# Rounded tile sizes and a written start order in a two-layer trunk kernel

## The chip, the cores and the metric

The kernel runs on one core of one Trainium2 chip. The metric is the device time of one execution in microseconds (us), as the median of several runs.

## The reference

`x` is 512 tokens of 1024 channels in fp32. Two residual layers follow each other. The first mixes tokens by a gated short convolution beside forgetting attention, the second by a conformer convolution module; a SwiGLU block follows each. Every sub-layer is normed ahead and behind. What the change touches is the beginning of the first mixer, cut here to its lines:

```python
def rms_norm(x, g):
    y = xf * lax.rsqrt(jnp.mean(xf * xf, axis=-1, keepdims=True) + RMS_EPS)
    return y * g

u = rms_norm(h, norm_mix_pre[layer])
proj = u @ w_in                      # gate B | gate C | xa | q | k | v | forget
log_f = log_sigmoid(proj[..., OFF_F:] + b_f)
y = concat([gate_b * conv3(gate_c * xa), attention(q, k, v, log_f)]) @ w_out
h = h + rms_norm(y, norm_mix_post[layer])
h = h + rms_norm(swiglu_ffn(rms_norm(h, norm_ffn_pre[layer])), norm_ffn_post[layer])
```

## The kernel before

Channels lie on the 128 partitions, eight tiles `h0` to `h7` of 128 x 512; tokens lie along the tile. Each fp32 factor is kept as a pair, a rounded high part and what is left (`xh` and `xl`, `wh` and `wl`), and each product is three matmuls (`mm3`, L198 to L200). The norm's factor per token isn't applied to `x` ahead of the product: `xh`, `xl` hold x times the gain, and the results are scaled by the factor later (`R`, spread over all partitions, and `rcol`, a column per 128 tokens).

Weights stream through `ensure` (L157 to L183): SyncE issues the transfer of a 512 KB chunk into `wr` (two buffers), ScalarE copies it rounded to `wh` (L176), and VectorE, for some chunks GpSimd, subtracts it for `wl` (L178, L181). For the first chunks of the start (`w_xa`) this is done in two halves.

The start of the program, in TensorE's order: `first()` has 32 units (k outer, four column blocks m inner) of three matmuls with `w_xa`; `forget()` has eight units of two matmuls (L425, L426) with the forget weights `wf`; `values()` has 32 units of three (L468 to L470) with `w_v`. Into this order `weave` puts other steps after a given number of units: `stats0` after STAT0 = 5 units of `forget()`, the norm's spread after STAT1 = 15 and the gate columns after GATES = 45. `stats0` sums the squares' columns with matmuls against a tile of ones (L258) in two halves of 256 tokens, each a group of two columns in the same PSUM bank `o`, the tag of which has one buffer. VectorE reads the two columns (L292, L293) and takes the root's inverse in Newton steps (L278, L283, L285). The squares are taken 256 wide on ScalarE (L248) and added 256 wide on GpSimd (L241).

TensorE's order is written by hand for the whole program. The order of ScalarE, VectorE, GpSimd and SyncE at the start is a scheduler's. In the later stages the tiles named `z` are streamed by TensorE too: they hold, among others, the hidden tiles of the SwiGLU blocks (outputs of L879 and its like). In the conformer stage (from 700 us) shifted copies of tiles are made by way of DRAM (`ct`, `uf`), and VectorE adds up the taps (L1015, L1132).

Tiles stand one behind the other in SBUF in the size that they ask for. Added up in that order, `xh`, `xl`, `wh`, `wl`, `wr` and `h` begin 64 bytes past a multiple of 128, the tiles `z0` to `z22`, `t` and `m` 32 bytes past it but for one.

Of the kernel before, what the change touches and what calls it, by code (L numbers as in the profile page):

```python
# [7 lines left out]
F32 = mybir.dt.float32  # L8
FR = mybir.dt.float32r
I32 = mybir.dt.int32  # L10
AF = mybir.ActivationFunctionType
ALU = mybir.AluOpType
AX = mybir.AxisListType

P = 128
T = 512
D = 1024
NK = D // P
NF = 22
HALF = NF // 2  # L20
TB = T // P
HT = T // 2
NH = 8
HD = 64
TAPS = 31
STAT0 = 5
STAT1 = 15
GATES = 45
LAG = 3
# [39 lines left out]
RMS_EPS = 1e-6  # L69
# [5 lines left out]
V_MIX_PRE = 0  # L75
# [14 lines left out]
def trunk(tc, x, vec, bands, w_xa, w_in, w_v, w_f, w_out, w_fi, w_fo, w_p1, w_p2, out):  # L90
# [5 lines left out]
    nc = tc.nc  # L96
    act = nc.scalar.activation
    tt = nc.vector.tensor_tensor
    ts = nc.vector.tensor_scalar
    stt = nc.vector.scalar_tensor_tensor  # L100
    mm = nc.tensor.matmul

    with tc.tile_pool(name="sb", bufs=1) as sb, tc.tile_pool(
        name="ps", bufs=1, space=bass.MemoryType.PSUM
    ) as pp, tc.tile_pool(name="dr", bufs=1, space=bass.MemoryType.DRAM) as dr:
        uid = [0]

        def alloc(tag, shape=(P, T), dt=F32, bufs=1):
            uid[0] += 1
            return sb.tile(list(shape), dt, name=f"{tag}_{uid[0]}", tag=tag, bufs=bufs)  # L110

        def psum(tag="g", shape=(P, T)):
            uid[0] += 1
            return pp.tile(list(shape), F32, name=f"p{tag}_{uid[0]}", tag=f"p{tag}", bufs=BANKS[tag])
# [5 lines left out]
        chunks = []  # L120
# [25 lines left out]
        for m in range(NK):  # L146
# [3 lines left out]
        count = {}  # L150
        pool_split = {(n, i) for n, w in (("p1", SPLIT1), ("p2", SPLIT2), ("in", SPLIT3), ("out", SPLIT4),
                                              ("fi", SPLIT5)) for i, c in enumerate(w) if c == "P"}
        split = []
        cursor = [0]
        spares = [None]

        def ensure(n, pieces=1):  # L157

            while len(split) < min(n, len(chunks)):
                name, ap, spare = chunks[len(split)]  # L160
                count[name] = count.get(name, -1) + 1
                raw = alloc("wr", (P, D), F32, 2)
                if spare is None:
                    h = alloc("wh", (P, D), FR, 5)
                    l = alloc("wl", (P, D), FR, 5)
                else:
                    if spare == 0:
                        spares[0] = alloc("pth", (P, 2560), FR), alloc("ptl", (P, 2560), FR)
                    h, l = (t[:, spare * D : (spare + 1) * D] for t in spares[0])
                a = ap.shape[1]  # L170
                r3 = raw.rearrange("p (a b) -> p a b", a=a)
                for i in range(pieces):
                    cs = slice(i * D // pieces, (i + 1) * D // pieces)
                    ps = slice(i * a // pieces, (i + 1) * a // pieces)
                    nc.sync.dma_start(r3[:, ps], ap[:, ps])
                    act(h[:, cs], raw[:, cs], AF.Copy)  # L176
                    if (name, count[name]) not in pool_split:
                        tt(out=l[:, cs], in0=raw[:, cs], in1=h[:, cs], op=ALU.subtract)  # L178
                        continue
                    for c in range(i * D // pieces, (i + 1) * D // pieces, HT):  # L180
                        nc.gpsimd.tensor_tensor(out=l[:, c : c + HT], in0=raw[:, c : c + HT], in1=h[:, c : c + HT],  # L181
                                                op=ALU.subtract)
                split.append((name, h, l))  # L183

        def take(name, ahead=2):
            i = cursor[0]
# [21 lines left out]
        ones = alloc("ones", (P, P), F32)  # L208
        nc.vector.memset(ones, 1.0)
        vecs = alloc("vecs", (P, NV), F32)  # L210

        def col(i, n=1):
            return vecs[:, i : i + n]
# [74 lines left out]
        def rsqrt_cols(sums, n, scale, eps):  # L288

            a = alloc("st_a", (P, 4), F32, 3)[:, :n]  # L290
            b = alloc("st_b", (P, 4), F32, 3)[:, :n]
            ts(out=a, in0=sums, scalar1=scale, scalar2=eps, op0=ALU.mult, op1=ALU.add)  # L292
            ts(out=b, in0=sums, scalar1=-0.5 * scale, scalar2=-0.5 * eps, op0=ALU.mult, op1=ALU.add)  # L293
            return newton(a, b, n)
# [31 lines left out]

        h = [alloc(f"h{k}") for k in range(NK)]
        nc.scalar.dma_start(vecs[:, : V_MIX_PRE + NK], vec[:, : V_MIX_PRE + NK])
        for k in range(NK):
            nc.sync.dma_start(h[k], x[:, k])  # L330
            if k % 2 == 0:
                ensure(k // 2 + 1, 2)
        wf_raw = slot(24, (P, NK * NH), F32)
        nc.sync.dma_start(wf_raw, w_f)
        nc.sync.dma_start(vecs[:, V_MIX_PRE + NK :], vec[:, V_MIX_PRE + NK :])
        wf = slot(25, (P, NK, 5, NH))

        def x_tiles():
# [5 lines left out]
            mm(warm[:, :P], ones, ones, start=True, stop=True)  # L344

        xh, xl = x_tiles()
        sums = Sums()
        for k in range(NK):
            g = col(V_MIX_PRE + k)
            ts(out=xh[k], in0=h[k], scalar1=g, scalar2=None, op0=ALU.mult)  # L350
            stt(out=xl[k], in0=h[k], scalar=g, in1=xh[k], op0=ALU.mult, op1=ALU.subtract)  # L351
            for hf in range(2):
                sums.square(hf, h[k][:, hf * HT : (hf + 1) * HT], k == NK - 1)
        wf3 = wf_raw.rearrange("p (k c) -> p k c", k=NK)
        act(wf[:, :, :4], wf3.unsqueeze(2).to_broadcast([P, NK, 4, NH]), AF.Copy)
        tt(out=wf[:, :, 4], in0=wf3, in1=wf[:, :, 0], op=ALU.subtract)
        R, R2 = alloc("R"), slot(23, dt=F32)
        rcol = alloc("rcol", (P, 4), F32)

        def stats0():  # L360
            for hf in range(2):
                nc.vector.tensor_copy(rcol[:, 2 * hf : 2 * hf + 2], rsqrt_cols(sums.cols(hf, "o"), 2, 1.0 / D, RMS_EPS))

        def stats1():
            act(R, spread(*each(rcol, 4)), AF.Copy)
# [14 lines left out]
        def first():  # L380

            ps = [psum("g") for _ in range(4)]
            for k in range(NK):
                if k % 2 == 0:
                    w = take("xa")
                for m in range(4):
                    mm3(ps[m], blk(w, k % 2 * 4 + m), (xh[k], xl[k]), k == 0, k == NK - 1)
                    yield
            for m in range(4):
                xa[m] = slot(2 * m, dt=F32)  # L390
                act(xa[m], ps[m], AF.Copy)
# [22 lines left out]
        def chain(*gens):  # L414
            for g in gens:
                yield from g
# [42 lines left out]
        def values():  # L459
            pv = [psum("g") for _ in range(TB)]  # L460
            for c in range(4):
                w = take("v")
                for j in range(2):
                    k = 2 * c + j
                    wh, wl = w[0][:, j * T : (j + 1) * T], w[1][:, j * T : (j + 1) * T]
                    for b in range(TB):
                        bs = slice(b * P, (b + 1) * P)
                        mm(pv[b], xh[k][:, bs], wh, start=k == 0, stop=False)  # L468
                        mm(pv[b], xh[k][:, bs], wl, start=False, stop=False)
                        mm(pv[b], xl[k][:, bs], wh, start=False, stop=k == NK - 1)  # L470
                        yield
            for b in range(TB):
                v4 = []
                for j in range(2):
                    w = slot(8 + 2 * b + j)
                    w4 = w.rearrange("p (e s d) -> p e s d", e=4, s=2)
                    p4 = pv[b][:, j * HT : (j + 1) * HT].rearrange("p (e d) -> p e d", e=4)
                    act(w4[:, :, 0], p4, AF.Copy, scale=rcol[:, b : b + 1])
                    stt(out=w4[:, :, 1], in0=p4, scalar=rcol[:, b : b + 1], in1=w4[:, :, 0],
                        op0=ALU.mult, op1=ALU.subtract)  # L480
                    v4.append(w)
                v.append(v4)
# [109 lines left out]
            stats1()  # L592
            gate_rows()

        weave(first())
        weave(chain(forget(), values()), [(STAT0, stats0), (STAT1, norm_known), (GATES, gate_cols)])

        def gemm_qk(i, j):
            return gemm("in", lambda ps: ev_qk(i, j, ps))
# [321 lines left out]
        g = {}  # L921
# [365 lines left out]
```

## Time and profile before

| | before |
|---|---|
| median of 3 runs | 1227.32 us (1225.16 to 1228.58) |
| profiled execution, its own time | 1230.15 us |
| span of the profiled execution | 1228.4 us |
| TensorE (PE) busy | 1178.8 us, 96% |
| VectorE (DVE) busy | 669.9 us, 55% |
| ScalarE (ACT) busy | 516.4 us, 42% |
| GpSimd (POOL) busy | 289.6 us, 24% |

The span runs from the first to the last instruction of the execution that was profiled; its own time lies 1.75 us above it. Busy is the time in which an engine works on some instruction. Matmuls overlap, so the distance between the starts of two of them tells more than the time of one.

### The profile page before, as it was taken

The page shows a single profiled execution, that of the slowest core. Times are in us where ns is not written, and L with a number is a line of the kernel's source. Part 1 is how long each engine was busy: PE and PEld are TensorE (multiplying, and loading weights), DVE is VectorE, ACT ScalarE, POOL GpSimd, SP SyncE. Part 2 cuts the span into 40 slices and gives each one's busy share as a digit, 9 for nine tenths or more (in the row PEclk, how much of TensorE's full clock was granted, in tenths as well). Part 3 has the DMA queues.
Part 4 walks back from the last instruction along what each step waited for, and adds up shares of the span by engine and source line. Part 5 has one row for each costly group of instructions (what it writes and reads, how often), then busy time and mean ns, then how long its engine had stood idle before and what let it go on. Part 6 is the DMA issues. An engine that isn't in the chain of part 4 may idle for free.

```text
span 1228.4 us, 16273 instructions
## 1 busy us (share of the span) xinstructions
PE 1178.8 (96%) x6134; PEld 997.8 (81%) x6134; DVE 669.9 (55%) x1240; ACT 516.4 (42%) x958; POOL 289.6 (24%) x373
## 2 busy tenths in 40 slices
PE   8899999989999999999999989899999999999994
PEld 6677777988888888888988878798888888888884
DVE  7568884375442234443378989827544323444416
ACT  4356774664232223322365664556433222332320
POOL 4244442741000000001545588046300000000010
PEclk9999999999999999999999999899999999999997
DMA  5332223414333233332313543022333323333212
GB/s 179 105 120 86 75 81 103 121 35 138 92 97 102 87 100 89 103 103 86 90 51 109 156 148 93 1 74 66 103 113 94 102 86 103 88 101 103 86 35 69
DMA packets 43118, 115.88 MB, mean 94 GB/s; under 512 B 4696, under 2 KB 14040, under 8 KB 43040
## 3 DMA queue, kind: packets, MB, share of 16 engines
q1 hardware_dynamic: 39936, 109.30, 29.9%
q10 hardware_dynamic: 2384, 3.15, 0.8%
q0 software_dynamic: 720, 2.39, 0.6%
q8 instruction: 48, 0.79, 0.3%
q14 instruction: 30, 0.25, 0.1%
HBM read 109.05 MB, written 5.78 MB: 93 GB/s over the span
## 4 chain that ended last, share of the span: by engine, by line
PE 75%; DVE 11%; DMA 4%; ACT 4%; POOL 3%; issue 3%; SPq 0%; DVEq 0%; ACTq 0%; POOLq 0%
PE pg L198 22%; PE pg L199 22%; PE pg L200 22%; DVE ps L1015 2%; PE pg L796 1%; PE pg L797 1%; DVE wl L178 1%; PE pp L561 1%; ACT wh L176 1%; DMA wr<-w_p 1%; POOL wl L181 1%; DMA wr<-w_fi 1%; POOL acc L241 1%; PE ps L540 1%; PE po L580 1%
## 5 line engine op out<-in xcount | busy, mean ns | idle before, releaser
L198 PE MATMUL pg<-xh,wh 128*128 128x512 f32 (+1 forms) x960 | 371.3, 387 | 0.1
L199 PE MATMUL pg<-xl,wh 128*128 128x512 f32 (+1 forms) x960 | 367.1, 382 | 3.1 <-DVE xl L351 3.1
L200 PE MATMUL pg<-xh,wl 128*128 128x512 f32 (+1 forms) x960 | 367.8, 383 | 1.0 <-DVE wl L178 1.0
L176 ACT ACTIVATE wh<-wr 128x1024 fp32r<-128x1024 f32 (+1 forms) x186 | 193.0, 1041 | 416.1 <-PE pg L199 331.0
L178 DVE TENSOR_TENSOR wl<-wr,wh 128x1024 fp32r<-128x1024 f32 (+1 forms) x145 | 176.1, 1216 | 178.5 <-ACT wh L176 178.0
L241 POOL TENSOR_TENSOR acc<-acc,sq 128x256 f32<-128x256 f32 x106 | 85.1, 815 | 720.5 <-ACT sq L248 719.2
L199 PEld LDWEIGHTS pg<-xl,wh 128*128 128x128 f32 x960 | 180.8, 188 | 37.6 <-DVE xl L351 3.8
L200 PEld LDWEIGHTS pg<-xh,wl 128*128 128x128 f32 x960 | 180.4, 188 | 37.6 <-DVE wl L178 2.0
L198 PEld LDWEIGHTS pg<-xh,wh 128*128 128x128 f32 x960 | 181.0, 189 | 34.5 <-issue 0.7
L198 PE MATMUL pg<-z,wh 128*128 128x512 f32 (+1 forms) x514 | 182.1, 354 | 0.0
L199 PE MATMUL pg<-z,wh 128*128 128x512 f32 (+1 forms) x514 | 181.0, 352 | 0.8 <-DVE z L411 0.8
L200 PE MATMUL pg<-z,wl 128*128 128x512 f32 (+1 forms) x514 | 181.1, 352 | 0.0
L181 POOL TENSOR_TENSOR wl<-wr,wh 128x256 fp32r<-128x256 f32 x164 | 132.7, 839 | 130.8 <-ACT wh L176 130.4
L199 PEld LDWEIGHTS pg<-z,wh 128*128 128x128 f32 x514 | 96.6, 188 | 15.6 <-DVE z L411 1.2
L198 PEld LDWEIGHTS pg<-z,wh 128*128 128x128 f32 x514 | 96.7, 188 | 14.7 <-ACT m L680 0.3
L200 PEld LDWEIGHTS pg<-z,wl 128*128 128x128 f32 x514 | 96.7, 188 | 14.4
L877 DVE TENSOR_TENSOR t<-pg,R 128x512 f32<-128x512 f32 (+1 forms) x48 | 31.0, 645 | 120.3 <-PE pg L200 120.3
L875 DVE TENSOR_TENSOR t<-pg,R 128x512 f32<-128x512 f32 (+1 forms) x48 | 31.0, 646 | 81.9 <-PE pg L200 79.4
L1015 DVE SCALAR_TENSOR_TENSOR ps<-z,vecs,ps 128x512 f32<-128x512 f32 x69 | 49.1, 750 | 0.6 <-ACT ps L1012 0.2
L796 PE MATMUL pg<-xh,wh 128*128 128x256 f32 x160 | 42.7, 294 | 1.2 <-ACT xh L1188 1.2
L879 ACT ACTIVATE z<-t 128x512 fp32r<-128x512 f32 (+1 forms) x48 | 28.7, 598 | 34.6 <-DVE t L878 34.6
L797 PE MATMUL pg<-xh,wl 128*128 128x256 f32 x160 | 42.2, 291 | 0.0
(257 smaller groups left out, 1433.0 us busy)
## 6 DMA issues: line engine op xcount, KB each, us to landing
wr<-w_fi SPq DMA_DIRECT2D x88, 512.0 KB
wr<-w_fo SPq DMA_DIRECT2D x44, 512.0 KB
wr<-w_p SPq DMA_DIRECT2D x24, 512.0 KB
wr<-w_in SPq DMA_DIRECT2D x16, 512.0 KB
wr<-w_out SPq DMA_DIRECT2D x8, 512.0 KB
h<-x SPq DMA_DIRECT2D x8, 256.0 KB
wr<-w_xa SPq DMA_DIRECT2D x8, 256.0 KB
wr<-w_v SPq DMA_DIRECT2D x4, 512.0 KB
```

What stands on the lines that cost most here:

```text
L176: act(h[:, cs], raw[:, cs], AF.Copy)
L178: tt(out=l[:, cs], in0=raw[:, cs], in1=h[:, cs], op=ALU.subtract)
L181: nc.gpsimd.tensor_tensor(out=l[:, c : c + HT], in0=raw[:, c : c + HT], in1=h[:, c : c + HT], op=ALU.subtract)
L198: mm(ps, wh, xh, start=first, stop=False)
L199: mm(ps, wh, xl, start=False, stop=False)
L200: mm(ps, wl, xh, start=False, stop=last)
L241: eng.tensor_tensor(out=acc, in0=acc, in1=t, op=ALU.add)
L796: mm(ps, wh, xt[0][k][:, cs], start=k == 0 and m % 2 == 0, stop=False)
L797: mm(ps, wl, xt[0][k][:, cs], start=False, stop=False)
L875: tt(out=tg, in0=pg, in1=R[:, cs], op=ALU.mult)
L877: tt(out=tu, in0=pu, in1=R[:, cs], op=ALU.mult)
L1015: stt(out=a if j < n - 1 else res, in0=u[:, j : j + T], scalar=w_col(i, j), in1=a, op0=ALU.mult, op1=ALU.add)
```

## The change

Three things. Each tile of 128 partitions takes a size that is rounded up to 128 bytes, so all of them begin at a multiple of 128. The start of the first layer is written in a fixed order for ScalarE, VectorE and GpSimd too: `xh` of k = 1 to 7 is made by ScalarE, squares are taken 512 wide by ScalarE, and they are added 512 wide by VectorE; GpSimd does none of it. And `stats0` sums all four columns as one group in one bank, and stands inside `first()`, after 27 of its units.

```diff
-STAT0 = 5
+STAT0 = 27
+LINE = 128
         def alloc(tag, shape=(P, T), dt=F32, bufs=1):
             uid[0] += 1
-            return sb.tile(list(shape), dt, name=f"{tag}_{uid[0]}", tag=tag, bufs=bufs)
+            n = int(np.prod(shape[1:]))
+            room = -(-4 * n // LINE) * LINE // 4
...
+            t = sb.tile([P, room], dt, name=f"{tag}_{uid[0]}", tag=tag, bufs=bufs)[:, :n]
...
-        def ensure(n, pieces=1):
+        def load(pieces=1):
...
                 nc.sync.dma_start(r3[:, ps], ap[:, ps])
+                yield
                 act(h[:, cs], raw[:, cs], AF.Copy)
...
-        for k in range(NK):
-            nc.sync.dma_start(h[k], x[:, k])
-            if k % 2 == 0:
-                ensure(k // 2 + 1, 2)
...
-        for k in range(NK):
-            g = col(V_MIX_PRE + k)
-            ts(out=xh[k], in0=h[k], scalar1=g, scalar2=None, op0=ALU.mult)
-            stt(out=xl[k], in0=h[k], scalar=g, in1=xh[k], op0=ALU.mult, op1=ALU.subtract)
-            for hf in range(2):
-                sums.square(hf, h[k][:, hf * HT : (hf + 1) * HT], k == NK - 1)
+        def begin():
+            for k in range(NK):
+                g = col(V_MIX_PRE + k)
+                nc.sync.dma_start(h[k], x[:, k])
+                if k % 2 == 0:
+                    halves = load(2)
+                next(halves)
+                if k == 3:
+                    nc.sync.dma_start(wf_raw, w_f)
+                    nc.sync.dma_start(vecs[:, V_MIX_PRE + NK :], vec[:, V_MIX_PRE + NK :])
+                if k:
+                    act(xh[k], h[k], AF.Copy, scale=g)
+                else:
+                    ts(out=xh[k], in0=h[k], scalar1=g, scalar2=None, op0=ALU.mult)
+                stt(out=xl[k], in0=h[k], scalar=g, in1=xh[k], op0=ALU.mult, op1=ALU.subtract)
+                next(halves, None)
+                if k % 2:
+                    next(halves, None)
+                sq = alloc("t", bufs=3) if k else sums
+                act(sq, h[k], AF.Square)
+                if k:
+                    tt(out=sums, in0=sums, in1=sq, op=ALU.add)
...
         def stats0():
-            for hf in range(2):
-                nc.vector.tensor_copy(rcol[:, 2 * hf : 2 * hf + 2], rsqrt_cols(sums.cols(hf, "o"), 2, 1.0 / D, RMS_EPS))
+            ps = psum("o", (P, TB))
+            for j in range(TB):
+                mm(ps[:, j : j + 1], sums[:, j * P : (j + 1) * P], ones[:, 0:1], start=j == 0, stop=j == TB - 1)
+            nc.vector.tensor_copy(rcol, rsqrt_cols(ps, TB, 1.0 / D, RMS_EPS))
...
-        weave(first())
-        weave(chain(forget(), values()), [(STAT0, stats0), (STAT1, norm_known), (GATES, gate_cols)])
+        with tc.manual_schedule(engines={mybir.EngineType.Activation, mybir.EngineType.DVE, mybir.EngineType.Pool}):
+            begin()
+            weave(first(), [(STAT0, stats0)])
+        weave(chain(forget(), values()), [(STAT1, norm_known), (GATES, gate_cols)])
```

On TensorE before, the column sums stand between the fifth and the sixth unit of `forget()` (`pp` is its result, `po` the bank of the sums):

```order
L425 MATMUL pp_345<-xh_32_147,z_26_131 40x512
L426 MATMUL pp_345<-xl_40_155,z_26_131 40x512
L258 MATMUL po_356<-ones_72,acc_161 128x1 x2
L258 MATMUL po_376<-ones_72,acc_161 128x1 x2
L425 MATMUL pp_345<-xh_33_148,z_26_131 40x512
L426 MATMUL pp_345<-xl_41_156,z_26_131 40x512
```

In the change these rows stand among the last units of `first()`, where lines 219 to 221 are what L198 to L200 were; nothing else moves on TensorE.

On VectorE before, from the last `xl` of the first layer (L351) to the second half of the sums (L292 and L293 read the bank `po`):

```order
L351 SCALAR_TENSOR_TENSOR xl_43_158<-h_12_82,vecs_74,xh_35_150 128x512
L178 TENSOR_TENSOR wl_120<-wr_118,wh_119 128x512 x2
L178 TENSOR_TENSOR wl_279<-wr_277,wh_278 128x1024
L178 TENSOR_TENSOR wl_309<-wr_307,wh_308 128x1024
L178 TENSOR_TENSOR wl_408<-wr_406,wh_407 128x1024
L178 TENSOR_TENSOR wl_461<-wr_459,wh_460 128x1024
L292 TENSOR_SCALAR st_a_359<-po_356 128x2
L293 TENSOR_SCALAR st_b_360<-po_356 128x2
```

And of the change, the same place (line 379 is what L351 was, 196 what L178 was, 386 the add of L241, 313 and 314 the read of the bank):

```order
L379 SCALAR_TENSOR_TENSOR xl_31_112<-h_12_82,vecs_74,xh_23_104 128x512
L196 TENSOR_TENSOR wl_185<-wr_183,wh_184 128x512
L386 TENSOR_TENSOR acc_113<-acc_113,t_200 128x512
L389 TENSOR_TENSOR z_14_85<-z_13_84,z_14_85 128x8x8
L196 TENSOR_TENSOR wl_259<-wr_257,wh_258 128x1024
L196 TENSOR_TENSOR wl_289<-wr_287,wh_288 128x1024
L313 TENSOR_SCALAR st_a_307<-po_302 128x4
L314 TENSOR_SCALAR st_b_308<-po_302 128x4
L299 TENSOR_SCALAR st_y_311<-st_a_307 128x4
L304 SCALAR_TENSOR_TENSOR st_u_312<-st_y_311,st_b_308 128x1 x4
L196 TENSOR_TENSOR wl_377<-wr_375,wh_376 128x1024
```

The read of the bank has moved from behind four 1024 wide subtractions of `w_v` to behind two, and a third and a fourth now stand between and behind the Newton steps. On SyncE the first transfers before are `h0`, both halves of `w_xa`'s first chunk, `h1`, `h2`; now they are `h0`, the first half, `h1`, the second half, `h2`. In the conformer stage SyncE issued, before, four loads of `z22` ahead of the four stores of `ct1`, and now those stores, the chunk of `w_p` and the load of `m5` go ahead of the loads of `z23` and `z22`.

## Rows read from the trace of the kernel before

**Rows 1.** The page: span, busy time and share of each engine.

```profile
span 1228.4 us, 16273 instructions
PE 1178.8 (96%) x6134; PEld 997.8 (81%) x6134; DVE 669.9 (55%) x1240; ACT 516.4 (42%) x958; POOL 289.6 (24%) x373
```

**Rows 2.** Windows of the start: busy (count) by engine, clock, DMA share, GB/s.

```profile
5.20:32.30 27.10, 23.48 (x99) 18.15 (x98) 21.50 (x27) 11.71 (x24) 12.08 (x13) 1.00 0.54 171
34.70:39.90 5.20, 0.44 (x5) 0.35 (x3) 2.68 (x5) 4.06 (x6) 0.00 (x0) 1.00 0.50 163
39.90:43.40 3.50, 3.45 (x11) 2.17 (x12) 3.09 (x17) 1.06 (x1) 1.34 (x2) 0.52 0.55 170
```

**Rows 3.** Timeline of TensorE: start, duration, line, [idle before <-releaser].

```profile
5.35 0.75 PE L198 MATMUL pg<-xh,wh 128*128 128x512 f32 x1
...
10.77 0.50 PE L199 MATMUL pg<-xl,wh 128*128 128x512 f32 x1 [1.60 <-DVE xl L351]
...
28.01 0.39 PE L200 MATMUL pg<-xh,wl 128*128 128x512 f32 x1
...
32.32 0.40 PE L425 MATMUL pp<-xh,z 128*40 128x512 f32 x1
...
34.64 0.50 PE L258 MATMUL po<-ones,acc 128*128 128x1 f32 x4
39.95 0.88 PE L258 MATMUL po<-ones,acc 128*128 128x1 f32 x4 [4.81 <-DVE st_y L278]
40.69 0.63 PE L425 MATMUL pp<-xh,z 128*40 128x512 f32 x1
...
43.25 0.51 PE L468 MATMUL pg<-wh,xh 128*128 128x512 f32 x1
...
48.14 1.05 PE L318 MATMUL ps<-eye,rcol 128*128 128x128 f32 x8
```

**Rows 4.** Timeline of TensorE in the first SwiGLU block, a gapless stretch of `z` tiles.

```profile
427.68 0.40 PE L198 MATMUL pg<-z,wh 128*128 128x512 f32 x1
...
432.35 0.40 PE L200 MATMUL pg<-z,wl 128*128 128x512 f32 x1
```

**Rows 5.** Groups of instructions by form, TensorE: count | busy us, mean ns | idle before.

```profile
L199 PE MATMUL pg<-xl,wh 128*128 128x512 f32 x896 | 349.0, 390 | 3.1 <-DVE xl L351 3.1
L199 PE MATMUL pg<-z,wh 128*128 128x512 f32 x318 | 126.0, 396 | 0.8 <-DVE z L411 0.8
L199 PE MATMUL pg<-z,wh 128*128 128x256 f32 x196 | 55.0, 280 | 0.0
L797 PE MATMUL pg<-xh,wl 128*128 128x256 f32 x160 | 42.2, 291 | 0.0
```

**Rows 6.** Timeline of VectorE at the start (a row can hold several instructions).

```profile
4.19 0.75 DVE L351 SCALAR_TENSOR_TENSOR xl<-h,vecs,xh 128x512 fp32r<-128x512 f32 x1
5.20 1.34 DVE L178 TENSOR_TENSOR wl<-wr,wh 128x512 fp32r<-128x512 f32 x2 [0.25 <-ACT wh L176]
8.07 0.49 DVE L350 TENSOR_SCALAR xh<-h,vecs 128x512 fp32r<-128x512 f32 x1 [1.54 <-DMA h<-x]
...
9.51 2.36 DVE L351 SCALAR_TENSOR_TENSOR xl<-h,vecs,xh 128x512 fp32r<-128x512 f32 x2
...
38.44 1.23 DVE L178 TENSOR_TENSOR wl<-wr,wh 128x1024 fp32r<-128x1024 f32 x1 [1.37 <-ACT wh L176]
39.59 0.15 DVE L292 TENSOR_SCALAR st_a<-po 128x2 f32<-128x2 f32 x1
```

**Rows 7.** Timeline of ScalarE at the start.

```profile
15.98 0.62 ACT L176 ACTIVATE wh<-wr 128x512 fp32r<-128x512 f32 x1
...
34.76 1.06 ACT L176 ACTIVATE wh<-wr 128x1024 fp32r<-128x1024 f32 x1 [3.64 <-DMA wr<-w_v]
...
37.35 1.06 ACT L176 ACTIVATE wh<-wr 128x1024 fp32r<-128x1024 f32 x1
```

**Rows 8.** Timeline of VectorE in the conformer stage.

```profile
715.34 1.05 DVE L1132 TENSOR_TENSOR z<-m,m 128x512 f32<-128x512 f32 x1 [3.44 <-DMA m<-ct]
```

More of the change, by code (lines that the diff above doesn't have):

```diff
@@ L109, in alloc @@
             uid[0] += 1
-            return sb.tile(list(shape), dt, name=f"{tag}_{uid[0]}", tag=tag, bufs=bufs)
+            n = int(np.prod(shape[1:]))
+            room = -(-4 * n // LINE) * LINE // 4
+            if shape[0] < P or room == n:
+                assert room == n
+                return sb.tile(list(shape), dt, name=f"{tag}_{uid[0]}", tag=tag, bufs=bufs)
+            t = sb.tile([P, room], dt, name=f"{tag}_{uid[0]}", tag=tag, bufs=bufs)[:, :n]
+            if len(shape) == 2:
+                return t
+            names = "abcd"[: len(shape) - 1]
+            return t.rearrange(f"p ({' '.join(names)}) -> p {' '.join(names)}", **dict(zip(names, shape[1:])))
         def psum(tag="g", shape=(P, T)):
@@ L155, in trunk @@
         spares = [None]
-        def ensure(n, pieces=1):
[L159 to L180, printed above, removed]
@@ new lines, in load @@
+        def load(pieces=1):
+            name, ap, spare = chunks[len(split)]
+            count[name] = count.get(name, -1) + 1
+            on_pool = (name, count[name]) in pool_split
+            raw = alloc("wr", (P, D), F32, 2)
+            if spare is None:
+                h = alloc("wh", (P, D), FR, 5)
+                l = alloc("wl", (P, D), FR, 5)
+            else:
+                if spare == 0:
+                    spares[0] = alloc("pth", (P, 2560), FR), alloc("ptl", (P, 2560), FR)
+                h, l = (t[:, spare * D : (spare + 1) * D] for t in spares[0])
+            split.append((name, h, l))
+            a = ap.shape[1]
+            r3 = raw.rearrange("p (a b) -> p a b", a=a)
+            for i in range(pieces):
+                cs = slice(i * D // pieces, (i + 1) * D // pieces)
+                ps = slice(i * a // pieces, (i + 1) * a // pieces)
+                nc.sync.dma_start(r3[:, ps], ap[:, ps])
+                yield
+                act(h[:, cs], raw[:, cs], AF.Copy)
+                if on_pool:
+                    for c in range(cs.start, cs.stop, HT):
@@ L181, in ensure @@
                         nc.gpsimd.tensor_tensor(out=l[:, c : c + HT], in0=raw[:, c : c + HT], in1=h[:, c : c + HT],
                                                 op=ALU.subtract)
-                split.append((name, h, l))
+                else:
+                    tt(out=l[:, cs], in0=raw[:, cs], in1=h[:, cs], op=ALU.subtract)
+                if i < pieces - 1:
+                    yield
+        def ensure(n):
+            while len(split) < min(n, len(chunks)):
+                for _ in load():
+                    pass
@@ L328, in trunk @@
         nc.scalar.dma_start(vecs[:, : V_MIX_PRE + NK], vec[:, : V_MIX_PRE + NK])
-        for k in range(NK):
-            nc.sync.dma_start(h[k], x[:, k])
-            if k % 2 == 0:
-                ensure(k // 2 + 1, 2)
         wf_raw = slot(24, (P, NK * NH), F32)
-        nc.sync.dma_start(wf_raw, w_f)
-        nc.sync.dma_start(vecs[:, V_MIX_PRE + NK :], vec[:, V_MIX_PRE + NK :])
         wf = slot(25, (P, NK, 5, NH))
@@ L346, in trunk @@
         xh, xl = x_tiles()
-        sums = Sums()
-        for k in range(NK):
-            g = col(V_MIX_PRE + k)
-            ts(out=xh[k], in0=h[k], scalar1=g, scalar2=None, op0=ALU.mult)
-            stt(out=xl[k], in0=h[k], scalar=g, in1=xh[k], op0=ALU.mult, op1=ALU.subtract)
-            for hf in range(2):
-                sums.square(hf, h[k][:, hf * HT : (hf + 1) * HT], k == NK - 1)
-        wf3 = wf_raw.rearrange("p (k c) -> p k c", k=NK)
-        act(wf[:, :, :4], wf3.unsqueeze(2).to_broadcast([P, NK, 4, NH]), AF.Copy)
-        tt(out=wf[:, :, 4], in0=wf3, in1=wf[:, :, 0], op=ALU.subtract)
+        sums = alloc("acc", bufs=2)
+        def begin():
[10 more added lines that the diff above has]
+                    act(xh[k], h[k], AF.Copy, scale=g)
+                else:
+                    ts(out=xh[k], in0=h[k], scalar1=g, scalar2=None, op0=ALU.mult)
[7 more added lines that the diff above has]
+                    tt(out=sums, in0=sums, in1=sq, op=ALU.add)
+            wf3 = wf_raw.rearrange("p (k c) -> p k c", k=NK)
+            act(wf[:, :, :4], wf3.unsqueeze(2).to_broadcast([P, NK, 4, NH]), AF.Copy)
+            tt(out=wf[:, :, 4], in0=wf3, in1=wf[:, :, 0], op=ALU.subtract)
         R, R2 = alloc("R"), slot(23, dt=F32)
```

## The prediction

> **What bounds the kernel now.** I read the busy times first, then the windows of the start, then TensorE's timeline at the places where a window falls short. TensorE is busy 1178.8 of 1228.4 us, and no other engine has more than 55% [rows 1]. So two things can move the time: gaps on TensorE, and the distance between two matmuls that follow each other without a gap.
>
> The gaps that the change touches lie in the first 43.4 us. [...] The timeline has the same in single matmuls: in an undisturbed stretch 19 matmuls take 32.32 - 28.01 = 4.31 us, 0.2268 each; at k=1 there is a wait of 1.60 us for `xl`; the second half of the column sums waits 4.81 us; and then a matmul of 512 columns takes 0.427 us (six from 40.69 to 43.25, where `values()` begins) [rows 3]. By the groups the waits for `xl` come to 3.1 us in all [rows 5].
>
> The distance differs with the tile that is streamed. `xh` and `xl` give the 0.2268 above; `z` tiles give (432.35 - 427.68) / 20 steps = 0.2335 us [rows 4]. The means by form agree in sign (390 ns against 396, with modelled ends), and of the 512 wide ones there are 3 x 896 with `xh`/`xl` and 3 x 318 with `z`, as each product's three lines have the same count [rows 5].
>
> **The start, `first()`.** Before, it takes from 5.35 to 32.32, 26.97 us, against 96 x 0.2268 = 21.77 without a gap: 5.2 us are lost [rows 3]. What is late is VectorE's work. `xl` of k=1 and 2 begins only at 9.51 and takes 1.18 us each, where the first took 0.75; GpSimd, idle at the first and busy 12.08 us of the window, does its adds beside them [rows 2, 6]. The change takes `xh` and the sums off the crowded places: per k ScalarE now has three 512 wide passes (0.62 us each by the copy at 15.98, so 1.9 us) and VectorE three (0.75 + 0.67 + 0.67 = 2.1 us, at the durations of the first `xl` and of the first pair of subtractions), against 4 x 3 x 0.2268 = 2.72 us for TensorE [rows 3, 6, 7]. Both stay ahead from k=2 on, so the later waits go. What is late next is k=1: the second half of `w_xa`'s first chunk is now issued behind `h1`, so I let it land when `h1` did before, at 8.07 [rows 6]; its copy (0.62) ends at 8.69, and TensorE, which comes to k=1 at 5.35 + 12 x 0.2268 = 8.07, loses 0.6, with the subtraction behind it some 0.7 us. Bounds: 0 (it lands earlier, as it isn't behind `h2`) and 1.6 us (the wait of k=1 in [rows 3] stays as it is). `first()` gains 5.2 - 0.7 = 4.5, between 3.6 and 5.2.
>
> **The column sums.** Before, four matmuls of the first half wait for nothing, but the second half needs the one bank, which VectorE frees by reading it, and VectorE's read at 39.59 stands behind a 1024 wide subtraction that began at 38.44 and waited for ScalarE's copy of `w_v` [rows 3, 6]. ScalarE in turn had waited 3.64 us for a chunk to land, and came to that copy at 37.35 [rows 7]. Now one bank takes all four columns, in one group, and nothing on TensorE waits for a read of it. The four matmuls stand after the unit k=6, m=2. They need the last add: 8 x 2.1 us of VectorE after 4.19, if it never waits, is 21.0; TensorE comes there at about 5.35 + 0.7 + 27 x 0.680 = 24.4. So 3.4 us of cover; should the landing of the last `h` use it up, each us beyond is a us lost, with the lower clock behind it. The stand-still and what hangs on it go: from 34.64 to 40.69, 6.05 us, becomes about 0.4 (four such matmuls took 40.69 - 39.95 = 0.74 at the lower clock); the six matmuls from 40.69 to 43.25, 2.56 us, become 6 x 0.232 = 1.39, by the ten from 32.32 to 34.64 [rows 3]. That is 5.65 + 1.2 = 6.8 us. Bounds: 6 and 7.
>
> Behind it Newton's steps still stand among the subtractions of `w_v` on VectorE. Their result, `rcol`, is first read by the spread at 48.14, 4.9 us after `values()` began [rows 3]; after the change that is near 32 + 4.9 = 36.9. The last `w_v` chunk's copy ran at 37.35; its buffer comes free earlier by at least the 4.5 us that `first()` gains, since VectorE's splitting now leads TensorE, so it runs near 33 at the latest, and the subtraction, 1.23 us as at 38.44, ends near 35.3 [rows 6, 7]. Cover 1.6 us or more; I cost it at nothing.
>
> 4.5 + 6.8 = 11.3; I take **11**, as small excesses follow every wait that is left. From `values()` on, TensorE's own order is unchanged, and its inputs are paced by it, so I let the 11 us carry to the end.
>
> **The rounding.** The streamed matmul reads a tile whose address the change moves. Added up from the tile sizes in the pool's order, `xh`, `xl`, `wh`, `wl` stood 64 bytes past a multiple of 128 and all but a few `z` 32 bytes past; all stand at 0 now. The trace has no matmul with both operands at 0. Bounds: the nearest rows are 0.2268 and 0.2335 us [rows 3, 4], and below them half of the 0.427 at the lower clock, 0.213. I take 0.2268 for all, because `z` is the one at the oddest offset: 954 x 6.7 ns = 6.4 us less. The 256 wide forms show no such loss with `z` (280 ns against 291), so I count nothing gained there, and half a us lost if they come to the spacing of the others [rows 5]. Sum: **6**. [...]
>
> **The conformer stage.** The scheduler, given other sizes and times, moves the shifted copies: `ct1` now goes ahead of four `z22` loads, so `m5` returns earlier. Before, VectorE waited there 3.44 us for that transfer [rows 8]. VectorE feeds TensorE there. I take 1 us of gain; bounds -3 and +3, as `z22` comes later by the same.
>
> **Sum.** 11 + 6 + 1 = 18. The profiled execution has a span of 1228.4 and took 1230.15, 2.8 us over the median of the runs, 1227.3; the changes are differences, so I take them from the median: **1209 us**.
>
> **The rivals.**
> 1. *The rounding does nothing.* Two like streams may differ for another reason than the address (what VectorE and ScalarE write at that time, or the weights' place). Then 1227.3 - 12 = 1215.
> 2. *All 512 wide matmuls gain.* If 64 bytes past cost something too, the 3642 of them could come down to 0.213: 13.5 ns x 3642 = 49 us, 1160; half of that is 1185. For it: 0.2268 is more than half of 0.427, though the clock is doubled. Against it: the gapless stretch of `xh` holds the same distance from matmul to matmul, which looks like a floor. [...]
> 3. *The stream of `xh` slows.* If `xh` and `wh` at the same offset 0 are worse than at 64, and as bad as `z` now, 2688 x 6.7 ns = 18.0 us are added and `z` gains nothing: 1215 + 18 = 1233, slower. It decides from (1231 - 1215) / 2688 = 6 ns on, that is at 0.233 us. For it: nothing in the trace ranks 0 above 64. Against it: `xh` at 64 is already faster than `z` at 32, so the rows that there are favour the rounder address.
> 4. *A new wait at `values()`' eviction.* The fourth eviction of `xa`'s banks on ScalarE stands behind the copy of `w_v`'s last chunk, which waits for a transfer [rows 7]; with the copy at 33 at the latest, the eviction (0.62) is done at 34.7, and the bank is wanted by the fourth block of `values()`, near 32 + 9 x 0.227 = 34.0. If the copy lags by 3 us more, 3.7 us are lost, and if the 1 us of the conformer turns to a loss of 3 besides, 7.7: 1213 to 1217.
>
> **How the numbers follow.** Forecast 0.54 (1205 to 1213), rival 1 0.14, rival 2 0.18, rival 3 0.10, rival 4 0.04. Two runs of this kernel that differ by under 0.3% (3.7 us) can't be told apart. Forecast, 1, 2 and 4 are faster, 0.90; of rival 3, 0.04 ends within 0.3% (3 to 6 ns) and 0.06 slower. The range leaves out the lower half of rival 2 and most of rival 3: 1178 to 1224.
>
> **What would show it.** In the profile after: TensorE's wait at k=1 under a us and none of over 0.3 at k=2 to 7; the four sums inside `first()` without a wait; `values()` from about 32; the granted clock 1.00 through 45 us; `z` streams at 0.227 and `xh` streams unchanged. If `xh` streams move at all, by 5 ns or more, the number is wrong by over 13 us, and that is the most likely way for it to be wrong; next comes `z` staying at 0.2335.

## The result and the profile after

The changed kernel takes 1211.27 us as the median of four runs (1209.95 to 1212.68), the kernel before 1227.51: ratio 0.9865, 95% interval 0.9851 to 0.9878. That is 16.2 us less; 1209 was forecast. Every ratio below is taken in the same way, to the kernel before on the same chip. The profiled executions differ by more, 19.9 us of span, since that of before lay 2.6 us over its median and that of after 1.1 under.

The first lines of the page:

```profile
span 1208.5 us, 16248 instructions
PE 1169.2 (97%) x6134; PEld 993.7 (82%) x6134; DVE 660.6 (55%) x1231; ACT 518.7 (43%) x957; POOL 278.3 (23%) x361
```

The windows of the start, columns as in [rows 2]:

```profile
5.20:28.30 23.10, 23.03 (x106) 18.73 (x105) 18.13 (x33) 16.90 (x29) 0.10 (x1) 1.00 0.71 229
28.30:32.30 4.00, 4.00 (x19) 2.08 (x18) 3.37 (x13) 2.35 (x4) 0.00 (x0) 1.00 0.63 208
32.30:43.40 11.10, 11.10 (x55) 9.29 (x54) 4.34 (x8) 4.23 (x6) 2.85 (x5) 1.00 0.41 114
```

TensorE is busy through all three, its clock stays at 1.00, and GpSimd works 0.10 us in the first. Its timeline, which answers to [rows 3] (L219 to L221 are what L198 to L200 were, 397 the sums, 461 `forget()`, 504 `values()`, 339 the spread):

```profile
5.56 0.50 PE L219 MATMUL pg<-xh,wh 128*128 128x512 f32 x1
...
6.62 0.39 PE L219 MATMUL pg<-xh,wh 128*128 128x512 f32 x1
...
24.33 0.95 PE L397 MATMUL po<-ones,acc 128*128 128x1 f32 x8
25.14 0.49 PE L219 MATMUL pg<-xh,wh 128*128 128x512 f32 x1
...
28.68 0.40 PE L461 MATMUL pp<-xh,z 128*40 128x512 f32 x1
...
32.40 0.39 PE L504 MATMUL pg<-wh,xh 128*128 128x512 f32 x1
...
37.17 1.05 PE L339 MATMUL ps<-eye,rcol 128*128 128x128 f32 x8
```

No row of this stretch has a wait on VectorE. `first()` takes 28.68 - 5.56 = 23.1 us in place of 27.0, `forget()` 3.7 in place of 10.9 with its sums, and `values()` begins at 32.40 instead of 43.25. What fed it, VectorE (386 adds the squares, 313 reads the bank, 398 writes `rcol`), answers to [rows 6]:

```profile
20.09 0.68 DVE L386 TENSOR_TENSOR acc<-acc,t 128x512 f32<-128x512 f32 x1
...
26.16 0.15 DVE L313 TENSOR_SCALAR st_a<-po 128x4 f32<-128x4 f32 x1
...
32.30 0.16 DVE L398 COPY rcol<-st_y 128x4 f32<-128x4 f32 x1
```

and ScalarE (190 copies weights, 427 evicts), which answers to [rows 7]:

```profile
7.21 0.63 ACT L190 ACTIVATE wh<-wr 128x512 fp32r<-128x512 f32 x1 [0.34 <-DMA wr<-w_xa]
...
30.07 1.06 ACT L190 ACTIVATE wh<-wr 128x1024 fp32r<-128x1024 f32 x1 [0.97 <-DMA wr<-w_v]
31.03 0.58 ACT L427 ACTIVATE z<-pg 128x512 f32<-128x512 f32 x1
```

The last add ends 3.5 us ahead of the sums, the fourth eviction 2.8 us ahead of the fourth block of `values()` (32.40 + 9 x 0.227), `rcol` 4.7 us ahead of the spread. The spacing of matmuls, first by form, as in [rows 5], then TensorE's timeline at the place of [rows 4]:

```profile
L220 PE MATMUL pg<-xl,wh 128*128 128x512 f32 x896 | 348.8, 389 | 0.0
...
L220 PE MATMUL pg<-z,wh 128*128 128x512 f32 x318 | 124.6, 392 | 0.8 <-DVE z L447 0.8
```

```profile
413.43 0.39 PE L219 MATMUL pg<-z,wh 128*128 128x512 f32 x1
...
415.47 0.39 PE L219 MATMUL pg<-z,wh 128*128 128x512 f32 x1
...
416.15 0.40 PE L219 MATMUL pg<-z,wh 128*128 128x512 f32 x1
...
418.94 0.39 PE L219 MATMUL pg<-z,wh 128*128 128x512 f32 x1
...
419.63 0.39 PE L219 MATMUL pg<-z,wh 128*128 128x512 f32 x1
...
420.10 0.39 PE L221 MATMUL pg<-z,wl 128*128 128x512 f32 x1
```

`xh` and `xl` stream as before; the `z` stream takes (420.10 - 415.47) / 20 = 0.2315 us here, against 0.2335 before and 0.2268 forecast. So the rounding gave a part of what was expected of it. (The rows between these two are taken up at the end of the experiments.) The wait in the conformer stage, [rows 8], is no shorter:

```profile
699.44 1.32 DVE L1170 TENSOR_TENSOR z<-m,m 128x512 f32<-128x512 f32 x1 [4.23 <-DMA m<-ct]
```

### The profile page after: what moved, and what is told of

Read it like the earlier page. It is cut to its first block, busy times and chain, and to the rows that moved or that the text cites. A ratio compares the mean times of both kernels' runs of the same rounds, so it can differ in the third digit from the quotient of the medians.

```text
span 1208.5 us, 16248 instructions
## 1 busy us (share of the span) xinstructions
PE 1169.2 (97%) x6134; PEld 993.7 (82%) x6134; DVE 660.6 (55%) x1231; ACT 518.7 (43%) x957; POOL 278.3 (23%) x361
## 4 chain that ended last, share of the span: by engine, by line
PE 76%; DVE 10%; POOL 4%; ACT 4%; DMA 3%; issue 3%; SPq 0%; ACTq 0%; POOLq 0%; DVEq 0%
PE pg L219 23%; PE pg L221 22%; PE pg L220 22%; DVE ps L1053 2%; PE pg L834 1%; DMA wr<-w_fi 1%; PE pg L835 1%; PE pp L597 1%; POOL acc L262 1%; POOL wl L193 1%; PE ps L576 1%; POOL z L1016 1%; DMA wr<-w_p 1%; PE po L616 1%; DVE xl L741 1%
## 5 line engine op out<-in xcount | busy, mean ns | idle before, releaser
L219 PE MATMUL pg<-xh,wh 128*128 128x512 f32 (+1 forms) x960 | 371.0, 386 | 0.1
L221 PE MATMUL pg<-xh,wl 128*128 128x512 f32 (+1 forms) x960 | 367.5, 383 | 0.5 <-DVE wl L196 0.5
L220 PE MATMUL pg<-xl,wh 128*128 128x512 f32 (+1 forms) x960 | 366.9, 382 | 0.0
L262 POOL TENSOR_TENSOR acc<-acc,sq 128x256 f32<-128x256 f32 x94 | 73.3, 789 | 706.5 <-ACT sq L269 705.1
L221 PEld LDWEIGHTS pg<-xh,wl 128*128 128x128 f32 x960 | 180.4, 188 | 37.1 <-DVE wl L196 1.3
L219 PEld LDWEIGHTS pg<-xh,wh 128*128 128x128 f32 x960 | 180.9, 188 | 34.2 <-issue 0.7
L220 PEld LDWEIGHTS pg<-xl,wh 128*128 128x128 f32 x960 | 180.7, 188 | 33.6
L219 PE MATMUL pg<-z,wh 128*128 128x512 f32 (+1 forms) x514 | 181.0, 352 | 0.0
L220 PE MATMUL pg<-z,wh 128*128 128x512 f32 (+1 forms) x514 | 179.7, 350 | 0.8 <-DVE z L447 0.8
L221 PE MATMUL pg<-z,wl 128*128 128x512 f32 (+1 forms) x514 | 179.8, 350 | 0.0
L220 PEld LDWEIGHTS pg<-z,wh 128*128 128x128 f32 x514 | 96.9, 188 | 14.5 <-DVE z L447 1.3
L219 PEld LDWEIGHTS pg<-z,wh 128*128 128x128 f32 x514 | 96.9, 188 | 13.6 <-ACT m L718 0.4
L221 PEld LDWEIGHTS pg<-z,wl 128*128 128x128 f32 x514 | 96.7, 188 | 13.4
```

The source lines that it names most:

```text
L219: mm(ps, wh, xh, start=first, stop=False)
L220: mm(ps, wh, xl, start=False, stop=False)
L221: mm(ps, wl, xh, start=False, stop=last)
L262: eng.tensor_tensor(out=acc, in0=acc, in1=t, op=ALU.add)
```

## The experiments

**The parts by themselves.** My theory at this point: the start is worth 11 us, the rounding some 4 by way of `z`, the rest is the conformer stage. Rivals: the rounding does nothing, or does something else. First the rounding alone, in the kernel before:

```diff
 def alloc(tag, shape=(P, T), dt=F32, bufs=1):
-    return sb.tile(list(shape), dt, ...)
+    room = -(-4 * n // 128) * 128 // 4
+    t = sb.tile([P, room], dt, ...)[:, :n]
...
```

> The kernel before with the rounded tile sizes alone; start and column sums as before. My theory: the start is unchanged (values() from about 43), the streams of z come to the spacing that they have in the changed kernel, 4 us less in all, and the conformer stage, whose SyncE order follows the rounding, gives about 1: 1222.5 us. Rival: the conformer stage is worth the 5 us that the two profiles differ by there, 1218. Rival: rounding does nothing to the time and the matmul spacing had another cause: 1227.

Measured: 1222.0 us against 1226.06, ratio 0.9966 (0.9949 to 0.9984). Of `z`, by form, and the start by windows:

```profile
L210 PE MATMUL pg<-z,wh 128*128 128x512 f32 x318 | 124.6, 392 | 0.8 <-DVE z L422 0.8
```

```profile
39.90:43.40 3.50, 3.50 (x11) 1.99 (x10) 3.50 (x16) 1.65 (x2) 2.31 (x4) 0.60 0.41 139
```

The 392 ns of the changed kernel, and the low clock at the start still there, a mean of 0.60 in this window. So alone the rounding gains 4.1 us, about the 3.7 ns by which the three `z` lines' means fell (397, 396, 396 to 394, 392, 392) times 954 = 3.5. The interval of the ratio spans some 2 to 6 us of gain; it is the means that tell 3.5 from the 6 that were forecast.

Next the changed kernel without the rounding:

```diff
-LINE = 128
+LINE = 4
```

> The changed kernel without the rounding (LINE = 4); the written start and the one-bank sums stay. My theory: values() starts near 32.4 as with the change, 11 us earlier than before, z streams at 0.2335 and the conformer stage as before: 1216 us. Rival: the rounding also speeds the start (copies and subtractions of aligned tiles), then values() starts later than 33 and the time is over 1218.

Measured: 1227.91 us, ratio 1.0016 (1.0001 to 1.0031): nothing is left of the gain. The start has it; the first row is that of `values()`, the others a gapless stretch of `xh` in the first SwiGLU block, on TensorE:

```profile
32.98 0.39 PE L504 MATMUL pg<-wh,xh 128*128 128x512 f32 x1
...
479.80 0.39 PE L220 MATMUL pg<-xl,wh 128*128 128x512 f32 x1
...
483.55 0.40 PE L221 MATMUL pg<-xh,wl 128*128 128x512 f32 x1
```

and by form:

```profile
L220 PE MATMUL pg<-xl,wh 128*128 128x512 f32 x896 | 355.0, 396 | 0.0
```

`values()` begins at 32.98, 10.3 us earlier than before, but `xh` and `xl` stream at 3.75 / 16 = 0.2344 us. The three means are 401, 396 and 396 ns against 394, 390 and 389 with the rounding: 6.7 ns x 2688 = 18 us, which is more than the start gained; `z` gives back some 2. By these means the kernel should be some 6 us slower than before, and it is 2. In the trace the 1920 of these matmuls that stand in the four stretches of the SwiGLU blocks account for 14.3 us: from the first 512 wide `xh` matmul of a stretch to the `z` matmul behind its last, the four take 452.9 us in all, 438.6 with the rounding. The others stand in the mixer and in the conformer stage, where TensorE waits for other things too; that the rest of their loss hides behind such waits is argued, not shown. The theory that was written down fell, and so did the rival's reason, since the start is as early as it should be. What differs is where tiles stand: the written start takes its tiles in another order, and unrounded, `wh` and `wl` then lie 32 bytes past a multiple of 512 and `xh`, `xl` at 448, where they had been 192 and 448 in the kernel before. These offsets, and all below, are remainders of a start address modulo 512 bytes, added up from the tile sizes in the order in which the program first asks for the tiles; no trace shows an address.

Third, one bank for the sums in the kernel before, all else as it was:

```diff
 def stats0():
-    for hf in range(2):
-        nc.vector.tensor_copy(rcol[:, 2 * hf : 2 * hf + 2], rsqrt_cols(sums.cols(hf, "o"), 2, 1.0 / D, RMS_EPS))
+    ps = psum("o", (P, TB))
+    for j in range(TB):
+        mm(ps[:, j : j + 1], sums.acc[:, j * P : (j + 1) * P], ones[:, 0:1], start=j == 0, stop=j == TB - 1)
+    nc.vector.tensor_copy(rcol, rsqrt_cols(ps, TB, 1.0 / D, RMS_EPS))
```

> The kernel before with the four column sums as one group in one bank alone, still after five units of forget(). My theory: the 4.8 us wait goes and the clock stays high, so values() starts near 36.4; but Newton's steps still begin at 39.6 behind the subtractions, so rcol is ready near 43 and the spread, due near 41.3, waits 1 to 2 us, and an eviction may cost 0.5: gain 4 to 5.5 us, 1222 to 1223.5. Rival: the whole 6.8 us stay: 1220.5. Rival: the wait only moves to the spread with its lower clock: under 2 us gained.

Measured: 1225.52 us, ratio 0.9990 (0.9976 to 1.0004), no change that can be told. TensorE's timeline (363 are the sums, 470 `values()`, 318 the spread):

```profile
34.40 0.95 PE L363 MATMUL po<-ones,acc 128*128 128x1 f32 x8
...
36.60 0.39 PE L470 MATMUL pg<-wh,xh 128*128 128x512 f32 x1
...
44.52 1.16 PE L318 MATMUL ps<-eye,rcol 128*128 128x128 f32 x8 [2.99 <-DVE rcol L364]
...
46.37 0.63 PE L470 MATMUL pg<-wh,xh 128*128 128x512 f32 x1
```

and VectorE, on which the read of the bank (L292) still stands behind a subtraction that waits for ScalarE's copy:

```profile
37.74 1.23 DVE L178 TENSOR_TENSOR wl<-wr,wh 128x1024 fp32r<-128x1024 f32 x1 [1.52 <-ACT wh L176]
38.88 0.15 DVE L292 TENSOR_SCALAR st_a<-po 128x4 f32<-128x4 f32 x1
```

`values()` begins 6.65 us earlier, as the term said, but the wait turns up at the spread, 2.99 us of it, with the lower clock behind it (a mean of 0.83 from 40 to 49 us, durations of 0.63). The third outcome that was written down is the nearest: the one bank alone moves the wait, and it needs the earlier subtractions of the written start (the read stands at 26.16 there) to be worth its 6.8 us. Last of these, the place of the sums, in the changed kernel without the rounding:

```diff
-STAT0 = 27
+STAT0 = 5
-weave(first(), [(STAT0, stats0)])
-weave(chain(forget(), values()), [(STAT1, norm_known), (GATES, gate_cols)])
+weave(first())
+weave(chain(forget(), values()), [(STAT0, stats0), (STAT1, norm_known), (GATES, gate_cols)])
```

> The changed kernel without the rounding and with the sums back after five units of forget() (STAT0 = 5 in the second weave, ScalarE's and VectorE's order after the start left to the scheduler). My theory: the bank, not the place, made the wait, so the sums don't wait there either, and the time is that of the kernel without the rounding within 1 us, 1216 to 1217, unless rcol then comes too late for the spread. Rival: the early place is what counts, and 3 us or more are lost against it.

Measured: 1228.86 us, ratio 1.0022 (1.0008 to 1.0037), against 1.0016 with the early place; the intervals overlap.

```profile
30.72 0.95 PE L397 MATMUL po<-ones,acc 128*128 128x1 f32 x8
...
37.82 1.06 PE L339 MATMUL ps<-eye,rcol 128*128 128x128 f32 x8
```

Neither the sums nor the spread wait on TensorE here: with the written start and the one bank, the place makes no difference that can be told.

**Offsets.** The new theory S: what counts is how the streamed tile stands to the weights, not where it stands; A: its own offset counts; N: neither. The kernels are the changed one, with small gaps ahead of `x`, `w` and `z` tiles in place of the rounding (`end[0]` is the byte at which the tile before ends):

```diff
+def place(tag):
+    return 0
...
+if tag[0] in "xwz":
+    pad = (place(tag) - end[0]) % 512
+    if pad:
+        sb.tile([P, pad // 4], F32, name=f"gap_{uid[0]}", tag=f"gap_{uid[0]}")
...
```

With `return 0`, all of them at 0 modulo 512:

> The changed kernel with small gaps in SBUF in place of the rounding, so that all tiles that TensorE reads (x, weights, z) begin at 0 modulo 512. Theory S (a matmul streams at 0.2268 us when streamed tile and weights lie at the same offset modulo 256, and slower when not): the z streams that are still slow in the changed kernel (z8 to z15 and z20, by 5 to 8 ns a matmul) come to 0.2268, about 3 us less: 1208 us, while the conformer stage's order is another and may give or take 2. Theory A (only the streamed tile's own offset counts, 0 modulo 256 is fast): the same. Theory N (offsets don't matter, the z streams differ for another reason): z streams as in the changed kernel, 1211.

With `return 128`:

> As the kernel with all offsets 0, but all of them 128 modulo 512. Theory S: equal offsets, so x, weights and z stream at 0.2268 and the time is that of offset 0 within 2 us, near 1208. Theory A: 128 is a slow offset, as for z8 to z15 in the changed kernel, so 2688 matmuls with xh and xl take 0.233 to 0.234, 17 to 20 us more, 1228; z too, 1234.

With `return 32`:

> As the kernel with all offsets 0, but all of them 32 modulo 512. Theory S: equal offsets, all streams at 0.2268, near 1208. Theory A, and any by which a start off a multiple of 64 or 128 is slow in itself: x and z at 0.231 to 0.235, 1226 to 1234.

Measured: 1206.75, 1208.19 and 1210.34 us, ratios 0.9846 (0.9827 to 0.9866), 0.9854 (0.9833 to 0.9876), 0.9869 (0.9850 to 0.9887). By form, at 32, the most uneven place of the three (at 0 and 128 each of these means lies within 1 ns):

```profile
L229 PE MATMUL pg<-xl,wh 128*128 128x512 f32 x896 | 349.0, 389 | 0.0
L228 PE MATMUL pg<-z,wh 128*128 128x512 f32 x318 | 124.4, 391 | 0.0
L229 PE MATMUL pg<-z,wh 128*128 128x512 f32 x318 | 123.9, 390 | 0.8 <-DVE z L456 0.8
```

At all three offsets `xh` and `z` have the fast means. Theory A would have had `xh` slow at 128 and 32, 18 us more, and it falls. In TensorE's timeline at offset 0, the stretch of [rows 4]:

```profile
413.80 0.39 PE L228 MATMUL pg<-z,wh 128*128 128x512 f32 x1
...
418.33 0.39 PE L230 MATMUL pg<-z,wl 128*128 128x512 f32 x1
```

4.53 / 20 = 0.2265 us: about the 0.2268 that the prediction had taken for all `z`.

The least edit that tells S from the others is one unused tile in the kernel without the rounding:

```diff
+            if not split:
+                alloc("gap", (P, 40))
             raw = alloc("wr", (P, D), F32, 2)
```

> The changed kernel without the rounding (measured at 1227.9 us), with one unused tile of 160 bytes ahead of the weight buffers; nothing else differs. It moves the weights from 32 to 192 modulo 512, xh and xl stay at 448: the same modulo 256. Theory S: the 2688 matmuls with xh and xl, now at 0.234, come to 0.2268, 18 to 20 us less, and z8 to z15 (then at 448) too: 1207 to 1210. Theory A (the streamed tile's offset alone): xh stays where it is and so does the time, 1228. Theory N: 1228.

Measured: 1213.66 us, ratio 0.9890 (0.9870 to 0.9910), where the same kernel without the 160 bytes had 1.0016.

```profile
L222 PE MATMUL pg<-xl,wh 128*128 128x512 f32 x896 | 348.8, 389 | 0.0
...
L222 PE MATMUL pg<-z,wh 128*128 128x512 f32 x318 | 124.4, 391 | 0.8 <-DVE z L449 0.8
```

`xh` is fast again, and the edit gains 14 us (15 by the ratios): the SwiGLU stretches come back to 438.5 us, 14.4 less, and the 18 to 20 expected were too many. The expectation has `z8` to `z15` gain too, as they then stand at 448. But the gap shifts every tile that is first asked for behind it: `z0` to `z18` and `z20` to `z22` move by the same 160 bytes as the weights and keep their distance to them, and only that of `xh`, `xl` changes. The `z` streams hardly moved (391 ns in this line, 392 without the gap, and 396 and 393 in the other two, against 397 and 393), as any theory of distances asks. What goes against theory S in its form modulo 256 is that `z8` to `z15`, 256 past the weights in both kernels, are slow in both. Counted off by tile in the program's order, their matmuls take 0.2304 us on the average here and 0.2306 without the gap; those of `xh`, 256 past the weights here too, take 0.2271.

Then `xh` and `xl` alone moved in the kernel with all offsets 0, by `return 128 if tag[0] == "x" else 0`:

> As the kernel with all offsets 0 (1206.75 us), but xh and xl alone at 128 modulo 512; weights and z stay at 0. Theory S (streamed tile and weights at one offset are fast, others not): xh and xl streams at 0.231 to 0.235 us, 11 to 22 us more over 2688 matmuls, 1218 to 1228; z streams stay at 0.227. Rival: only a mixture of offsets within one stage makes streams slow, and xh, all at one offset, stay at 0.227: 1207.

and by `return 256 if tag[0] == "x" else 0`:

> As the kernel with all offsets 0, but xh and xl alone at 256 modulo 512. The kernel before had them 256 past the weights' offset and streamed at 0.2268, so by theory S modulo 256 they do so here: 1207. Rival: modulo 512 counts and the kernel before was fast for another reason: 1218 to 1228.

Measured: 1221.04 us, ratio 0.9965 (0.9951 to 0.9978), at 128, and 1208.47 us, ratio 0.9851 (0.9825 to 0.9876), at 256. By form at 128, then at 256:

```profile
L229 PE MATMUL pg<-xl,wh 128*128 128x512 f32 x896 | 353.9, 395 | 0.0
...
L229 PE MATMUL pg<-z,wh 128*128 128x512 f32 x318 | 124.0, 390 | 0.8 <-DVE z L456 0.8
```

```profile
L229 PE MATMUL pg<-xl,wh 128*128 128x512 f32 x896 | 349.1, 390 | 0.0
```

At 128 past the weights `xh` is slow and `z`, at the weights' offset, is not; at 256 past them `xh` is fast. That mixture within a stage is needed is thereby out: all `xh` stood alike.

Another rival was left. When tiles move, those that VectorE, ScalarE, GpSimd and the DMA queues read and write move as well, and their accesses could be what holds the stream up. The kept traces answer it. In the kernel without the rounding, and then in the changed one, this is a stretch of `xh` in which none of the three engines works (columns as in [rows 2]), with TensorE's first and last row of it:

```profile
434.80:438.10 3.30, 3.30 (x15) 2.64 (x14) 0.00 (x0) 0.00 (x0) 0.00 (x0) 1.00 0.49 159
434.82 0.39 PE L220 MATMUL pg<-xl,wh 128*128 128x512 f32 x1
...
438.10 0.39 PE L219 MATMUL pg<-xh,wh 128*128 128x512 f32 x1
```

```profile
428.80:431.90 3.10, 3.10 (x16) 2.56 (x15) 0.00 (x0) 0.00 (x0) 0.00 (x0) 1.00 0.56 169
428.72 0.39 PE L220 MATMUL pg<-xl,wh 128*128 128x512 f32 x1
...
431.89 0.39 PE L219 MATMUL pg<-xh,wh 128*128 128x512 f32 x1
```

That is 3.28 / 14 = 0.2343 and 3.17 / 14 = 0.2264 us, slow and fast as before. Over the whole of the two traces, the matmuls with `xh` or `xl` beside which no DMA worked either, 67 and 101 of them, keep a distance of 0.2341 and 0.2267 us. So no other engine's and no DMA's work holds the stream up here.

Equal offsets are not the whole rule either. TensorE's rows come in the order that the program writes (L219, L220, L221 in turn), so they can be counted off by tile: from 413.43 in the result's fence the changed kernel streams `z0` to `z21` in pairs, three matmuls a pair, with the weights at 256. `z0` to `z7`, at 256 too, take (416.15 - 413.43) / 12 = 0.2267 us; `z8` to `z15`, at 128, (418.94 - 416.15) / 12 = 0.2325; and `z16`, `z17`, again at the weights' 256, (419.63 - 418.94) / 3 = 0.230. Over all such blocks of the trace the last is 0.2317. With every tile alike, at 0, 32 or 128, these two take 0.2267. So a tile at the weights' offset can be slow among neighbours that are not; why `z16`, `z17` are and `z0` to `z7` aren't, no run here shows.

Last, the changed kernel and the one with all offsets 0 beside each other on one chip:

> The changed kernel once more, beside the kernel with all offsets 0 on the same chip: 1210 to 1212 us.

> The kernel with all offsets 0 once more, beside the changed kernel on the same chip. Theory S: its z streams give back 3 us of the changed kernel's, so 1207 to 1209, 2 to 4 us under it. Rival: the 4.5 us seen were the variation between executions and nothing is left: within 1 us.

Measured: 1211.96 us, ratio 0.9881 (0.9861 to 0.9901), and 1208.22, ratio 0.9850 (0.9828 to 0.9872). The 3.7 us between them fit the 2.5 us by the means of `z` (954 x 2.6 ns: 394, 392, 392 to 391, 390, 389), and the first pair, 1211.27 and 1206.75, has the same sign. Both pairs' intervals overlap a little, so that it beats the changed kernel is likely and not certain; that it beats the kernel before, by 1.5%, is.

## Why the prediction was right, point by point

The sum came out near, 18 us against 16.2, and the profile bears out its largest term, the start: the sums were due near 24.4, `values()` near 32 and the spread near 36.9, and they stand at 24.33, 32.40 and 37.17.

- `first()`: 4.5 us expected. It takes 23.12 us, 22.31 without the sums that now stand in it, against 26.97: 4.66. The wait at k=1 (0.7) didn't come, as the second half's copy began at 7.21, not 8.07; in its place the first triple lost 0.4 us (6.62 - 5.56 = 1.06, for 0.68). So the size is right, and the place of the half us that is left was not.
- The column sums: 6.8 expected. From the end of `first()` to `values()` it was 10.93 us and is 3.72, less the 0.81 that the sums take in `first()` (24.33 to 25.14): 6.4. I had given them 0.4; the four records of half the sums before were two columns, not four. Together 11.1, of which 0.2 went to a later first matmul (5.56 for 5.35), against 11. The reason given was half of it: one bank alone only moved the wait to the spread. The Newton steps, named and costed at nothing, are as much a condition; the written order ahead of them gave their cover.
- The rounding: 6 expected. This is the step that was mis-sized: 3.5 us by the means of `z`, and 4.1 in the run of the rounding alone. "I take 0.2268 for all" assumed that an offset of 0 modulo 128 is enough for `z`; in the changed kernel the weights stand at 256 modulo 512 and `z8` to `z15` at 128, and such a difference is slow (0.2325 above). Rival 1, which gave 1215, took two like streams to differ for another reason than the address; the kernels of one offset show that it is the address, and the stretches without work on other engines that it isn't what VectorE and ScalarE write. Against it stand also 389 ns for `xl` at the weights' offset and 395 at 128 past it (L229 with `wh`, all offsets 0 and `xh`, `xl` alone at 128).
- What the prediction didn't see: in this change the rounding is worth far more than its own term, since it keeps `xh` fast. It was costed against the layout of before, where `xh` was fast already, and not against the layout that the written start would have without it. Against that, it is worth 1227.9 - 1211.3 = 16.6 us (18.5 by the ratios 1.0016 and 0.9865). Parts that interact cannot be priced one by one from the kernel before. That "`xh` streams unchanged" came true is luck as far as the prediction goes: among multiples of 128 the distance between `xh` and the weights could also have come out as 128, and the kernel with `xh` alone there takes 1221.04 us against 1208.22 of the one with all at 0 on the same chip, 12.8 more. It came out as 256.
- Rival 3, `xh` as slow as `z`, had the price right, and that the address sets it (0.2335 forecast, 0.2344 in the kernel without the rounding, 18 us), and its condition wrong: it feared the same offset, and the slow `xh` stood at a different one.
- Rival 2: in none of the stretches shown did 512 wide matmuls follow each other under 0.2264 us, so it has no support here. Its 0.213 was an estimate, half of the 0.427 us that the kernel before took at a granted clock of 0.50 (40.20 to 43.20); no run shows it at 1.00. Rival 4: the fourth eviction had 2.8 us in hand.
- The conformer stage: 1 expected from a shorter wait. The wait was 4.23 us in place of 3.44, so that reason failed. What is left of the medians' 16.2 us after 10.9 and 3.5 is 1.8, and no run took that stage by itself. One profiled execution can't settle it: between two fixed places of TensorE's order (the first 512 wide `xh` matmul of the stage, and the first 256 wide one of `mm3` in it) it takes 163.9 us before and 159.1 after, but 162.4 when the changed kernel was profiled once more, and 162.1 and 156.1 in two profiles of the kernel with all offsets 0. Here are these last two from 715 to 790 us:

```profile
715.00:790.00 75.00, 67.12 (x444) 64.42 (x445) 60.98 (x142) 35.66 (x81) 33.33 (x36) 0.84 0.15 45
715.00:790.00 75.00, 66.94 (x485) 63.37 (x484) 60.90 (x142) 38.22 (x87) 32.42 (x36) 0.95 0.15 44
```

TensorE is busy for about as long in both and gets through 444 and 485 matmuls, at a mean granted clock of 0.84 and 0.95. One kernel thus differs from itself here by 3 to 6 us, more than the term. Most of the 3.7 us by which the profiled spans differ beyond the medians can lie here too. Whether the change gains anything in this stage stays open.

## What to carry to other kernels

When code is reordered, its buffers may be placed elsewhere: compare the distances between gapless matmuls before judging the new order, or a gain at one place is paid back a few nanoseconds at a time (6.7 here) at 2688 others. Put all streamed tiles of a stage and their weights at one offset, and not only some of them; all three common offsets tried were fast (389 to 391 ns for `xl` and `z`). Before a difference of a few us is given to a change, see how far one kernel differs from itself in that stage. When a wait is taken away, follow the data behind it to the next reader, as the spread shows: the work that made it late has to move too.

## What the runs showed of the hardware that was not expected

A matmul of 512 fp32r columns took 0.2265 to 0.2267 us from start to start when all streamed tiles and the weights began at one offset modulo 512 (0, 32 and 128 tried). With `xh` 256 past the weights it took 0.2264 in the changed kernel and 0.2268 in the one before, and the mean duration was 390 ns where `xh` alone had been moved so. With `xh` 128 past them the mean duration rose by 5 to 6 ns, and with `xh` at 448 and weights at 32 the distance was 0.2344. The loss was there with no other engine and no DMA at work (0.2341). The offset to the weights alone doesn't say it all: in the changed kernel `z16`, `z17` at the weights' own offset took 0.2317, among tiles at others. By what mechanism the offsets act, no run here tells.
